# The output projection as a plain product over quarters of x1, with its sums on VectorE

## The chip, the core and the metric

The kernel runs on one core of one Trainium2 chip. The metric is the device time of one execution in microseconds (us). The engines are PE (TensorE matmuls; PEld is its weight loads), DVE (VectorE), ACT (ScalarE), POOL (GpSimd) and SP (SyncE, which here issues every DMA). Each engine takes its instructions in one fixed order, which a list scheduler made when the kernel was built.

## What is computed

One layer of a decoder trunk over 1024 tokens of width 1024, all float32. Three gated mixers give y; then come the output projection and a feed-forward part:

```python
y = gates[..., 0, :] * o_mla + gates[..., 1, :] * o_gla + gates[..., 2, :] * o_mem
x = x + y @ w_o                                          # the output projection
h2 = rms_norm(x, g_ffn)
return x + jnp.square(jax.nn.relu(h2 @ w_up)) @ w_down   # 1024 -> 4096 -> 1024
```

Every float32 product is made of three matmuls over rounded parts: an operand is split into `hi` (a cast by ACT, line 135) and `lo` (the difference, a subtraction by DVE, line 136), and the three are hi·hi, hi·lo and lo·hi.

## The kernel before

The change lies at the seam between the memory branch, whose last matmuls are the tiles `om` (line 131), the output projection (`phase_out`) and the first column groups of the up product (`phase_up`). Tokens lie on the partitions in tiles of 128, so x has 8 tiles; y lies transposed, as 8 tiles `Y` of 128 features by 1024 tokens. `x1` is x plus half of y @ w_o.

**Projection.** y @ w_o is a product of 2 x 2 blocks of 512 x 512, made as seven block products in Winograd's form instead of eight: step s is product `order[s]`, adds into a PSUM bank per token tile (`multiply`, line 1292: 4 tiles x 4 feature tiles x 3 matmuls = 48 matmuls), and after each step DVE adds half of the bank to a quarter of x1 (line 1296). The operands of most products are sums of blocks of y or w_o. They are formed by POOL (`tt`, lines 1237 to 1263), then split by ACT and DVE into slots. Four banks are used for four token tiles at a time, so a step can only begin in a fresh bank when that bank's sum has been taken over.

**Turning.** As quarters of x1 are complete, `scale` (lines 1304 to 1311) gets each token's factor by ACT and POOL and scales the tokens, `turn` (lines 1320 and 1333) turns them by PE and ACT, and `split` makes the operands of the up product: "11", "22", "21", "t1", "t2", "t3", "t4".

**Up product.** It runs by groups of 256 columns of w_up, again with seven products p1 to p7 per group (`up_group`, line 1460, 12 matmuls of 512 columns each). The first three groups are interleaved in `phase_up`, since their later operands are ready last. Weights of a group come by two DMAs into `fraw` (three buffers, line 1418); four sums of their blocks are formed (`up_weights`, lines 1430 to 1443), then split. In a group p6 leaves a sum in bank b2; DVE takes it over (`fu`, line 1496) before p7 may add more into the same bank; then DVE makes `fv` and `fc` (lines 1501 and 1503) before p3 may add into b3.

Of the kernel before, what the change touches and what calls it, by code (L numbers as in the profile page):

```python
# [7 lines left out]
F32 = mybir.dt.float32  # L8
# [11 lines left out]
P = 128  # L20
S = 1024
D = 1024
# [79 lines left out]
class _Kernel:  # L102
# [1101 lines left out]
    def phase_out(self):  # L1204
# [8 lines left out]
        Y, W, T = self.Y, {}, {}  # L1213
        places = {"12": ["wraw", "wraw", "whi", "wlo"], "21": ["whi"] * 4, "22": ["wlo"] * 4, "11": ["ftmp"] * 4}
        for n in ("12", "21", "22", "11"):
            for k in range(4):
                r = W[n, k] = self.t512(places[n][k])
                i, j = int(n[0]) - 1, int(n[1]) - 1
                nc.sync.dma_start(r, wv[4 * j + k][:, so[i]])
        order = (2, 5, 3, 1, 6, 7, 4)  # L1220
        goes = {1: (0, 0), 5: (1, 1), 6: (0, 1), 3: (0, 1), 7: (1, 1), 2: (0, 0), 4: (1, 0)}
        fresh = (2, 5, 1)
        A, C = {}, {}
        plan = {0: (False, False), 1: (True, True), 2: (True, False), 3: (False, True), 4: (True, True),
                5: (False, False), 6: (True, True)}
        tt = pool.tensor_tensor

        def conv_act(s, ks):
            i = order[s]
            if s not in A:  # L1230
                A[s] = self.slots(plan[s][0])
            h, l = A[s]
            for k in ks:
                y11, y12, y21, y22 = Y[k][:, so[0]], Y[k][:, so[1]], Y[4 + k][:, so[0]], Y[4 + k][:, so[1]]
                if i == 5:
                    src = self.t512("flo")
                    tt(src, y12, y11, op=ALU.subtract)
                elif i == 6:
                    tt(y12, y22, y12, op=ALU.subtract)
                    tt(y11, y12, y11, op=ALU.add)  # L1240
                    src = y11
                elif i == 4:
                    tt(y21, y21, y11, op=ALU.subtract)
                    src = y21
                else:
                    src = {3: y22, 2: y21, 1: y11, 7: y12}[i]
                self.split_sb(h[:, k, :], l[:, k, :], src)

        def conv_w(s, ks):
            i = order[s]  # L1250
            if s not in C:
                C[s] = self.slots(plan[s][1])
            h, l = C[s]
            for k in ks:
                if i == 5:
                    src = T["s", k] = self.t512("fhi")
                    tt(src, W["21", k], W["22", k], op=ALU.add)
                elif i == 3:
                    s2 = T["s", k]
                    tt(s2, s2, W["11", k], op=ALU.subtract)  # L1260
                    src = self.t512("flo")
                    tt(src, W["12", k], s2, op=ALU.subtract)
                    tt(W["21", k], W["11", k], W["21", k], op=ALU.subtract)
                else:
                    src = T["s", k] if i == 6 else W[{2: "12", 1: "11", 7: "21", 4: "22"}[i], k]
                self.split_sb(h[:, k, :], l[:, k, :], src)

        conv_act(0, range(4))
        conv_w(0, range(4))
        conv_act(1, range(4))  # L1270
        x1 = []
        for t2 in range(4):
            xt = self.hp.tile([P, 2, D], F32, name="x1", tag="H", bufs=8)
            for i in range(2):
                nc.sync.dma_start(xt[:, i, :], a["x"][0, (2 * t2 + i) * P:(2 * t2 + i + 1) * P, :])
                x1.append(xt[:, i, :])
# [4 lines left out]
        banks = {}  # L1281

        def multiply(s, p):
            i = order[s]
            if i in fresh:
                banks[p] = self.bank([P, 512], ("x1", "x2")[p // 2])
            ps = banks[p]
            (ah, al), (wh, wl) = A[s], C[s]
            tok = slice(P * p, P * p + P)
            for k in range(4):  # L1290
                for m, (l, r) in enumerate(((ah, wh), (ah, wl), (al, wh))):
                    pe.matmul(ps, l[:, k, tok], r[:, k, :], start=(i in fresh and k + m == 0), stop=(k == 3 and m == 2),  # L1292
                              skip_group_check=i not in fresh)
            oh, th = goes[i]
            acc = x1[4 * th + p][:, so[oh]]
            dve.scalar_tensor_tensor(acc, ps, 0.5, acc, op0=ALU.mult, op1=ALU.add)
# [42 lines left out]
        N = len(order)  # L1339
# [24 lines left out]
        at(5, 0, begin, ("11", True))  # L1364
        for k in range(4):
            at(5, k // 2, lambda k=k: split("11", k, raw[0, 0, k]))
            at(5, 2 + k // 2, second, k)
        at(6, 0, begin, ("t1", False), ("22", False), ("t3", False))
        at(6, 0, spill, range(4, 8))
        for k in range(4):  # L1370
            at(6, k // 2, lambda k=k: split("t1", k, raw[0, 0, k]))
            at(6, 2 + k // 2, third, k)
        for s in range(N):
            for p in range(4):
                multiply(s, p)
                if p < 2:
                    if s + 1 < N:
                        conv_w(s + 1, (2 * p, 2 * p + 1))
                elif s + 2 < N:
                    conv_act(s + 2, (2 * p - 4, 2 * p - 3))  # L1380
                for f in extra.get((s, p), []):
                    f()
        scale(1, 0, (0, 1))
        scale(1, 0, (2, 3))
        spill(range(4))
        begin(("t2", True), ("21", True), ("t4", False))
# [3 lines left out]
        def last():  # L1390
            for k in range(4):
                split("t2", k, raw[0, 0, k])
# [7 lines left out]
    def up_part(self, g, i, w):  # L1400
# [7 lines left out]
        if i == 5:  # L1408
            self.pool.tensor_tensor(r[0], r[0], r[1], op=ALU.add)
        w[i] = self.ff_split(r[0])  # L1410

    def up_weights(self, g, w=None):
# [10 lines left out]
        tt = self.pool.tensor_tensor  # L1423
# [107 lines left out]
    def phase_up(self, a_dram, close):  # L1531
# [9 lines left out]
        with tc.tile_pool(name="f_tmp", bufs=1, side="right") as tmp:  # L1541
# [16 lines left out]
            for i in (6, 7):  # L1558
                g0[i]()
            self.up_weights(1, w1)  # L1560
            for i in (4, 3):
                g0[i]()
            for i in (6, 7):
                g1[i]()
            self.up_weights(2, w2)
            for i in (4, 3):
                g1[i]()
            w = self.up_weights(3)
            for i in (6, 5, 7, 4, 3):
                g2[i]()  # L1570
            for g in range(3, NG):
# [253 lines left out]
```

## Time and profile before

| | |
|---|---|
| median of 3 runs | 1960.88 us (1959.6 to 1961.91) |
| the profiled execution | 1963.93 us, of which the span of its trace is 1962.1 us |
| mean granted TensorE clock of that execution | 0.988 of full speed |
| PE busy | 1894.0 us, 97% of the span |
| DVE, ACT, POOL busy | 1222.1, 901.6 and 563.1 us |
| DMA | 185.83 MB, 95 GB/s over the span |

All times of rows are counted from the start of the span. "Busy" of PE counts each matmul from its start to its modelled end, so that overlapping matmuls count once. Where an engine sat idle, the trace names what ended the idle time.

### The profile page before, as it was taken

Reading aid. Unit: us, or ns where it says so; the run is one execution under the profiler, and the core shown is the slowest. Engines: PE = TensorE matmul, PEld = TensorE weight load, DVE = VectorE, ACT = ScalarE, POOL = GpSimd, SP = SyncE. Lnnn points to the kernel's source line nnn. Section 1 sums busy time; section 2 is a strip of 40 time slices with the busy share of each in tenths; the row PEclk is TensorE's granted clock in tenths of the full one; section 3 lists DMA queues with packets and bytes.
Section 4 is the critical chain, followed back from the end, with each engine's and each line's share of the span. In section 5 each row is a group of like instructions: output and inputs, shape, how many; then the busy total and the mean of one; then the engine's idle time right before and its main releaser. Section 6 shows DMA issues by size and latency. Waiting matters only on the chain. (4 is left out here: it accounts for less than half of the span.)

```text
span 1962.1 us, 28464 instructions
## 1 busy us (share of the span) xinstructions
PE 1894.0 (97%) x10330; PEld 1627.2 (83%) x10330; DVE 1222.1 (62%) x2125; ACT 901.6 (46%) x2125; POOL 563.1 (29%) x644
## 2 busy tenths in 40 slices
PE   7999999999999999999999998898999999999999
PEld 6889989899879798888988987576888887888887
DVE  7666464655656636364455446876756567698796
ACT  5465465554653323233244434375444546544432
POOL 2321313112124323232310125723322224244150
PEclk9999999999999999999999999899999999999999
DMA  4021110211111411112123114034545457745543
GB/s 144 25 65 49 30 52 28 62 47 48 38 55 34 139 44 43 43 44 73 31 62 113 43 36 150 17 118 124 182 135 161 141 166 247 241 131 187 182 137 118
DMA packets 141852, 185.83 MB, mean 95 GB/s; under 512 B 11352, under 2 KB 91744, under 8 KB 141712
## 3 DMA queue, kind: packets, MB, share of 16 engines
q1 hardware_dynamic: 141712, 184.02, 29.7%
q8 instruction: 81, 1.33, 0.3%
q14 instruction: 59, 0.48, 0.1%
HBM read 137.84 MB, written 46.14 MB: 94 GB/s over the span
## 5 line engine op out<-in xcount | busy, mean ns | idle before, releaser
L208 PE MATMUL mm<-H,whi 128*128 128x512 f32 x1280 | 411.2, 400 | 2.2 <-DVE g_rg L767 2.2
L208 PEld LDWEIGHTS mm<-H,whi 128*128 128x128 f32 x1280 | 232.5, 190 | 42.4 <-DVE g_rg L767 2.6
L208 PE MATMUL mm<-H,wlo 128*128 128x512 f32 x640 | 253.3, 396 | 0.0
L136 DVE TENSOR_TENSOR wlo<-wraw,whi 128x768 fp32r<-128x768 f32 (+3 forms) x134 | 113.4, 850 | 119.9 <-ACT whi L135 116.8
L208 PEld LDWEIGHTS mm<-H,wlo 128*128 128x128 f32 x640 | 121.1, 189 | 24.8
L135 ACT CAST whi<-wraw 128x768 fp32r<-128x768 f32 (+3 forms) x134 | 95.9, 721 | 94.0 <-PE mm L208 42.2
L131 PE MATMUL s<-whi,H 128*128 128x384 f32 x512 | 139.1, 346 | 0.0
L1679 PE MATMUL x<-h,h 128*128 128x512 f32 x528 | 121.8, 390 | 0.0
L1679 PEld LDWEIGHTS x<-h,h 128*128 128x128 f32 x528 | 99.1, 188 | 21.0
L221 PE MATMUL mm<-whi,H 128*128 128x256 f32 x512 | 95.7, 285 | 0.0
L131 PEld LDWEIGHTS s<-whi,H 128*128 128x128 f32 x512 | 93.4, 188 | 1.0 <-ACT whi L135 0.2
L1460 PE MATMUL b<-H,whi 128*128 128x512 f32 x272 | 86.9, 401 | 5.6 <-DVE fc L1503 4.3
L131 PE MATMUL s<-wlo,H 128*128 128x384 f32 x256 | 87.6, 342 | 0.2 <-DVE wlo L136 0.2
L221 PEld LDWEIGHTS mm<-whi,H 128*128 128x128 f32 x512 | 80.8, 192 | 0.3
L1460 PE MATMUL b<-h,whi 128*128 128x512 f32 x248 | 78.4, 396 | 1.1 <-ACT whi L135 1.1
L1460 PE MATMUL b<-H,fhi 128*128 128x512 f32 x240 | 74.5, 391 | 2.5 <-DVE fc L1503 2.5
L823 ACT ACTIVATE g_dd<-g_dd 128x1024 f32<-128x1024 f32 x28 | 29.6, 1058 | 100.1 <-POOL g_dd L822 100.1
L1687 DVE TENSOR_TENSOR acc<-x,acc 128x512 f32<-128x512 f32 x80 | 54.2, 683 | 32.6 <-PE x L1679 32.4
L221 PE MATMUL mm<-wlo,H 128*128 128x256 f32 x256 | 72.4, 283 | 0.0
L586 DVE TENSOR_REDUCE sst<-s 128x1 f32<-128x384 f32 (+4 forms) x96 | 52.8, 554 | 31.3 <-PE s L584 18.0
L1679 PE MATMUL x<-H,h 128*128 128x512 f32 x288 | 68.2, 395 | 0.0
L1679 PE MATMUL x<-h,H 128*128 128x512 f32 x288 | 68.1, 395 | 0.0
(455 smaller groups left out, 5064.4 us busy)
## 6 DMA issues: line engine op xcount, KB each, us to landing
wraw<-w_in SPq DMA_DIRECT2D x58, 384.0 KB, 3.4
a<-fc SPq DMA_DIRECT2D x80, 256.0 KB, 2.8
fraw<-w_up SPq DMA_DIRECT2D x32, 512.0 KB, 4.4
whi<-a SPq DMA_DIRECT2D x56, 256.0 KB, 4.0
wlo<-a SPq DMA_DIRECT2D x56, 256.0 KB, 3.8
x<-x SPq DMA_DIRECT2D x24, 512.0 KB, 5.8
dw<-x SPq DMA_DIRECT2D x32, 256.0 KB, 3.4
a<-wraw SPq DMA_DIRECT2D x30, 256.0 KB, 2.1
```

The lines of the kernel that those rows point to most:

```text
L131: self.pe.matmul(out, l, r, start=(i == 0), stop=(i == last))
L135: self.act.copy(hi, src)
L136: self.dve.tensor_tensor(lo, src, hi.bitcast(F32), op=ALU.subtract)
L208: self.pe.matmul(ps, l[:, c], r[:, tok], start=(k + i == 0), stop=(k == KT - 1 and i == 2))
L221: self.pe.matmul(ps[:, i, :], l[:, tok], r, start=(k + j == 0), stop=(k == KT - 1 and j == 2))
L586: self.dve.tensor_reduce(st[:, b:b + 1], sp[b][:, 0:n], axis=X, op=ALU.max, negate=True)
L823: act.activation(dd, dd, AF.Exp, scale=0.0625)
L1460: pe.matmul(ps[name], l[:, k, :], r[:, k, :], start=(not more and k + m == 0), stop=(k == 3 and m == 2), skip_group_check=more)
L1679: pe.matmul(ps, l[:, k, tok], r[:, k, :], start=(i in (1, 5, 2) and k + m == 0), stop=(k == 3 and m == 2), skip_group_check=i not in (1, 5 ...
L1687: dve.tensor_tensor(out, ps, out, op=ALU.add)
```

## The change

The projection becomes a plain product: eight steps instead of seven, each one half of the sum for a quarter of x1 (512 output columns by 512 tokens). Two steps follow each other in the same four banks, and DVE adds the banks to x1 only after the second. The operands are blocks of y and of w_o as they are; POOL forms no sums for them any more. The x1 tiles lie in the buffers of `Y`, the y operands keep the eight `H` slots. The scaling and turning of a quarter moves with its step. The sums for the up product's weights (in `up_part`, and in `up_weights` for the first three groups) and the one in `third` go from POOL to DVE. In `phase_up` the call that makes the next group's weights stands behind the products p6, p7, p4, p3 of the group before, where it stood between p7 and p4, so it has a lower priority than their evictions.

```diff
+        def weights(n):
+            i, j = int(n[0]) - 1, int(n[1]) - 1
+            r = [self.t512({"11": "wraw", "12": "fhi", "22": "ftmp", "21": "flo"}[n]) for _ in range(4)]
             for k in range(4):
...
+                nc.sync.dma_start(r[k], wv[4 * j + k][:, so[i]])
+            if n == "11":
+                W[n] = [[x[:, 0, :] for x in self.ff_split(x.unsqueeze(1))] for x in r]
+                return
+            hi, lo = self.slots(True)
...
+        def tokens(kh, th):
+            hi, lo = Y[kh, th] = self.slots(False)
+            for k in range(4):
+                self.split_sb(hi[:, k, :], lo[:, k, :], self.Y[4 * kh + k][:, so[th]])
...
+        weights("11")
+        tokens(0, 0)
+        tokens(0, 1)
...
+        load_x1(range(4))
+        tokens(1, 0)
+        weights("12")
+        tokens(1, 1)
+        load_x1(range(4, 8))
+        weights("22")
+        weights("21")
...
+        steps = [(oh, th, kh) for oh, th, khs in ((0, 0, (0, 1)), (0, 1, (0, 1)), (1, 1, (1, 0)), (1, 0, (0, 1))) for kh in khs]
 
         def multiply(s, p):
-            i = order[s]
-            if i in fresh:
+            oh, th, kh = steps[s]
+            first = s % 2 == 0
+            if first:
                 banks[p] = self.bank([P, 512], ("x1", "x2")[p // 2])
...
+            if not first:
+                acc = x1[4 * th + p][:, so[oh]]
+                dve.scalar_tensor_tensor(acc, ps, 0.5, acc, op0=ALU.mult, op1=ALU.add)
...
-        for s, (oh, th) in ((4, (0, 0)), (5, (0, 1)), (6, (1, 1))):
+        for s, (oh, th) in ((2, (0, 0)), (4, (0, 1)), (6, (1, 1))):
...
-            tt(r12, r22, r12, op=ALU.subtract)
-            split("t3", k, r12)
+            dve.tensor_tensor(r12, r22, r12, op=ALU.subtract)
...
-            self.pool.tensor_tensor(r[0], r[0], r[1], op=ALU.add)
+            self.dve.tensor_tensor(r[0], r[0], r[1], op=ALU.add)
...
-        tt = self.pool.tensor_tensor
+        tt = (self.dve if had else self.pool).tensor_tensor
...
-            for i in (6, 7):
+            for i in (6, 7, 4, 3):
                 g0[i]()
             self.up_weights(1, w1)
-            for i in (4, 3):
-                g0[i]()
-            for i in (6, 7):
+            for i in (6, 7, 4, 3):
                 g1[i]()
             self.up_weights(2, w2)
-            for i in (4, 3):
-                g1[i]()
-            w = self.up_weights(3)
             for i in (6, 5, 7, 4, 3):
                 g2[i]()
+            w = self.up_weights(3)
```

The scheduler decides where this puts the instructions. On POOL, behind the last additions of the memory branch (`Y<-Y,m_y`), these rows stood before:

```order
L1237 TENSOR_TENSOR flo<-Y 128x512 [waits Pool_49] x2
L1138 TENSOR_TENSOR Y<-Y,m_y 128x512 [waits DVE_49]
L1237 TENSOR_TENSOR flo<-Y 128x512 [waits Pool_49]
L1257 TENSOR_TENSOR fhi<-whi,wlo 128x512 [waits DMAHW5_49,DMAHW4_49]
...
L1263 TENSOR_TENSOR whi<-ftmp,whi 128x512 [waits DMAHW1_49,Pool_49]
...
L1260 TENSOR_TENSOR fhi<-fhi,ftmp 128x512 [waits DVE_49]
L1239 TENSOR_TENSOR Y<-Y 128x512
L1262 TENSOR_TENSOR flo<-wraw,fhi 128x512 [waits DMAHW0_49,Pool_49]
```

Now the additions are followed by the small operations of `scale` alone:

```order
L1138 TENSOR_TENSOR Y<-Y,m_y 128x512 [waits DVE_49] x14
L1279 TENSOR_TENSOR f_q<-f_q,xms 128x2 [waits PE_49,Activation_49]
L1280 TENSOR_SCALAR f_q<-f_q 128x2 [waits Pool_49]
L1281 TENSOR_TENSOR f_sc<-f_q,mhalf 128x2 [waits Pool_49]
```

The 32 block sums of the projection are gone from POOL, and the last addition of the memory branch has no sum ahead of it. On SP, whose queue issues the loads, the second quarter of w_o (`fhi`, for the second step) now stands behind loads of x and of w_up:

```order
L1376 DMA wraw<-w_up 128x4x128 [waits DMAHW3_49,DVE_49]
L1242 DMA Y<-x 128x1024 [waits DVE_49,Pool_49]
L1242 DMA Y<-x 128x1024 [waits DVE_49] x2
L1376 DMA wraw<-w_up 128x4x128 [waits DMAHW4_49,DVE_49,Activation_49]
L1219 DMA fhi<-w_o 128x512 [waits DMAHW5_49,PE_49]
```

Before, the last quarter to be loaded (`ftmp`) stood behind loads of x alone:

```order
L1275 DMA x_12877<-x 128x1024 [waits DMAHW7_49]
L1275 DMA x_12880<-x 128x1024 [waits DMAHW0_49]
L1219 DMA ftmp<-w_o 128x512 [waits DVE_49,DMAHW1_49,PE_49,Activation_49]
L1219 DMA ftmp<-w_o 128x512 [waits DMAHW2_49]
```

So the load of `fhi` can't be issued until a buffer of `wraw` is free. On DVE, where group 0's p6 is taken over (`fu<-fs,b`), the order before was this; the four rows ahead of it split group 0's weights, and the sums are POOL's:

```order
L136 TENSOR_TENSOR flo<-ftmp,fhi 128x512
L136 TENSOR_TENSOR wlo<-ftmp,whi 128x512
L136 TENSOR_TENSOR flo<-fraw,fhi 128x512
L136 TENSOR_TENSOR wlo<-ftmp,whi 128x512
L1496 TENSOR_TENSOR fu<-fs,b_13872 128x512
```

Now, from the first of group 1's sums on (lines 1399, 1401, 1408 and 1412 are the four sums of a group):

```order
L1399 TENSOR_TENSOR ftmp<-fraw 128x512
L1401 TENSOR_TENSOR ftmp<-ftmp,fraw 128x512
L1408 TENSOR_TENSOR ftmp<-fraw 128x512
L1412 TENSOR_TENSOR ftmp<-fraw,ftmp 128x512
L136 TENSOR_TENSOR flo<-ftmp,fhi 128x512
L136 TENSOR_TENSOR wlo<-ftmp,whi 128x512
L136 TENSOR_TENSOR flo<-fraw,fhi 128x512
L136 TENSOR_TENSOR wlo<-ftmp,whi 128x512
L1399 TENSOR_TENSOR ftmp<-fraw 128x512
L1465 TENSOR_TENSOR fu<-fs,b_13818 128x512
L1401 TENSOR_TENSOR ftmp<-ftmp,fraw 128x512
```

Ahead of group 0's `fu` there stand now, besides group 0's own sums and splits, those of group 1 and the first sum of group 2, which waits for group 2's load.

## Rows read from the trace of the kernel before

**Rows 1.** The page: span, and PE's busy time, share and instructions.

```profile
span 1962.1 us, 28464 instructions
PE 1894.0 (97%) x10330; PEld 1627.2 (83%) x10330; DVE 1222.1 (62%) x2125; ACT 901.6 (46%) x2125; POOL 563.1 (29%) x644
```

**Rows 2.** Three stretches: projection, first three groups, later groups; columns named in row one.

```profile
core 0: us, PE busy (x) PEld busy (x) DVE busy (x) ACT busy (x) POOL busy (x), PEclk, DMA share, GB/s
1204.33:1317.55 113.22, 97.40 (x399) 74.40 (x398) 87.16 (x103) 54.09 (x106) 65.77 (x52) 0.91 0.28 98
1317.55:1395.09 77.54, 66.68 (x271) 51.60 (x270) 55.62 (x73) 43.46 (x76) 32.54 (x23) 0.93 0.44 139
1395.09:1560.00 164.91, 164.91 (x718) 134.48 (x717) 102.83 (x138) 80.20 (x135) 49.68 (x35) 1.00 0.48 152
```

**Rows 3.** PE's waits, 1204 to 1317.5: us in total, times, longest.

```profile
PE x L1292 <- DVE h L136: 4.7, 2, 4.4
PE x L1292 <- DVE x L1296: 3.8, 2, 2.7
PE x L1292 <- ACT H L135: 3.2, 2, 2.3
PE trs L1320 <- ACT ftmp L1311: 2.1, 2, 1.8
PE om L131 <- ACT m_ph L1124: 0.6, 1, 0.6
```

**Rows 4.** PE's instructions in order of time: start, us, line, tiles, count, idle before.

```profile
1226.10 13.25 PE L1292 MATMUL x<-h,h 128*128 128x512 f32 x44 [0.28 <-DVE h L136]
...
1304.04 1.04 PE L1320 MATMUL trs<-ident,ftmp 128*128 128x128 f32 x8
1304.83 8.47 PE L1292 MATMUL x<-h,h 128*128 128x512 f32 x36
...
1363.65 0.70 PE L1460 MATMUL b<-H,whi 128*128 128x512 f32 x2 [3.86 <-DVE fc L1503]
...
1368.07 0.63 PE L1460 MATMUL b<-h,fhi 128*128 128x512 f32 x2
```

**Rows 5.** DVE in order of time: a split beside POOL's sums, and with POOL idle.

```profile
1216.51 6.17 DVE L136 TENSOR_TENSOR h<-flo,h 128x512 fp32r<-128x512 f32 x4 [4.36 <-ACT h L135]
...
1268.07 2.48 DVE L136 TENSOR_TENSOR h<-fhi,h 128x512 fp32r<-128x512 f32 x4
```

**Rows 6.** POOL in order of time: the last two additions to Y.

```profile
1209.54 1.29 POOL L1138 TENSOR_TENSOR Y<-Y,m_y 128x512 f32<-128x512 f32 x1 [2.55 <-DVE m_y L1136]
...
1214.54 1.29 POOL L1138 TENSOR_TENSOR Y<-Y,m_y 128x512 f32<-128x512 f32 x1
```

**Rows 7.** DVE in order of time: the last m_y of the memory branch.

```profile
1210.87 0.69 DVE L1136 SCALAR_TENSOR_TENSOR m_y<-m_gate,om 128x512 f32<-128x512 f32 x1 [1.41 <-POOL Y L1138]
```

**Rows 8.** SP's issues in order of time: w_o, then fraw.

```profile
1209.98 1.94 SPq L1219 DMA_DIRECT2D ftmp<-w_o  x4
...
1340.04 1.05 SPq L1418 DMA_DIRECT2D fraw<-w_up  x2
```

**Rows 9.** DMA issues, 1170 to 1235: line, count, KB each, median us to landing.

```profile
ftmp<-w_o SPq DMA_DIRECT2D x4, 256.0 KB, 4.0
```

**Rows 10.** The loads of fraw, 1336 to 1400.

```profile
DMA to landing us min/median/max: 3.7/4.4/7.7
```

**Rows 11.** POOL in order of time: the first sum of group 0's weights.

```profile
1346.98 1.29 POOL L1430 TENSOR_TENSOR ftmp<-fraw 128x512 f32<-128x512 f32 x1 [23.77 <-DMA fraw<-w_up]
```

**Rows 12.** DVE, then ACT: the last read of Y's buffers; copies out of banks.

```profile
1337.41 0.68 DVE L1396 TENSOR_TENSOR flo<-flo,Y 128x512 f32<-128x512 f32 x1
...
1328.26 1.84 ACT L1333 ACTIVATE Y<-trs,vec 128x512 f32<-128x512 f32 x3 [1.42 <-PE trs L1320]
```

**Rows 13.** PE's waits, 1317.5 to 1395.1.

```profile
PE b L1460 <- DVE fc L1503: 4.3, 2, 3.9
PE trs L1320 <- ACT ftmp L1311: 2.8, 1, 2.8
```

More of the change, by code (lines that the diff above doesn't have):

```diff
@@ L1212, in phase_out @@
         so = [slice(0, 512), slice(512, 1024)]
[L1213 to L1215 removed]
+        T, Y, W = {}, {}, {}
+        def weights(n):
+            i, j = int(n[0]) - 1, int(n[1]) - 1
+            r = [self.t512({"11": "wraw", "12": "fhi", "22": "ftmp", "21": "flo"}[n]) for _ in range(4)]
             for k in range(4):
[L1217 to L1219 removed]
@@ L1220, in phase_out @@
[L1220 to L1228, printed above, removed]
-            i = order[s]
[L1230 to L1276, printed above, removed]
+                nc.sync.dma_start(r[k], wv[4 * j + k][:, so[i]])
+            if n == "11":
+                W[n] = [[x[:, 0, :] for x in self.ff_split(x.unsqueeze(1))] for x in r]
+                return
@@ new lines, in weights @@
+            hi, lo = self.slots(True)
+            W[n] = [(hi[:, k, :], lo[:, k, :]) for k in range(4)]
+            for k in range(4):
+                self.split_sb(*W[n][k], r[k])
+        def tokens(kh, th):
+            hi, lo = Y[kh, th] = self.slots(False)
+            for k in range(4):
+                self.split_sb(hi[:, k, :], lo[:, k, :], self.Y[4 * kh + k][:, so[th]])
+        self.fams = ["w"]
+        weights("11")
+        tokens(0, 0)
+        tokens(0, 1)
+        x1 = [None] * NT
@@ L1277, in phase_out, with load_x1 @@
+        def load_x1(ts):
+            for t in ts:
+                x1[t] = self.new_Y(F32)
+                nc.sync.dma_start(x1[t], a["x"][0, t * P:(t + 1) * P, :])
+        load_x1(range(4))
[5 more added lines that the diff above has]
+        weights("21")
         sm = self.small
@@ L1281, in phase_out @@
         banks = {}
+        steps = [(oh, th, kh) for oh, th, khs in ((0, 0, (0, 1)), (0, 1, (0, 1)), (1, 1, (1, 0)), (1, 0, (0, 1))) for kh in khs]
         def multiply(s, p):
-            i = order[s]
-            if i in fresh:
+            oh, th, kh = steps[s]
+            first = s % 2 == 0
+            if first:
                 banks[p] = self.bank([P, 512], ("x1", "x2")[p // 2])
             ps = banks[p]
-            (ah, al), (wh, wl) = A[s], C[s]
+            ah, al = Y[kh, th]
             tok = slice(P * p, P * p + P)
-            for k in range(4):
+            for k, (wh, wl) in enumerate(W[f"{oh + 1}{kh + 1}"]):
                 for m, (l, r) in enumerate(((ah, wh), (ah, wl), (al, wh))):
[L1292 to L1296, printed above, removed]
+                    pe.matmul(ps, l[:, k, tok], r, start=(first and k + m == 0), stop=(not first and k == 3 and m == 2))
+            if not first:
+                acc = x1[4 * th + p][:, so[oh]]
+                dve.scalar_tensor_tensor(acc, ps, 0.5, acc, op0=ALU.mult, op1=ALU.add)
         def scale(oh, th, js):
@@ L1337, in spill @@
                 nc.sync.dma_start(self.x_dram[t], x1[t])
-        N = len(order)
+        N = len(steps)
         extra = {}
@@ L1363, in begin @@
                 B[n] = self.slots(own)
-        at(5, 0, begin, ("11", True))
-        for k in range(4):
[L1366 to L1369, printed above, removed]
+        at(4, 0, begin, ("11", True))
+        at(5, 1, begin, ("t1", False))
+        at(6, 0, spill, range(4, 8))
+        at(6, 0, begin, ("22", False))
+        at(7, 0, begin, ("t3", False), ("t2", True))
+        for k in range(4):
+            at(4, 2 + k // 2, lambda k=k: split("11", k, raw[0, 0, k]))
+            at(5, k // 2, second, k)
+            at(5, 2 + k // 2, lambda k=k: split("t1", k, raw[0, 0, k]))
+            at(6, 2 + k // 2, third, k)
+            at(7, k // 2, lambda k=k: split("t3", k, raw[0, 1, k]))
+            at(7, 2 + k // 2, lambda k=k: split("t2", k, raw[0, 0, k]))
         for k in range(4):
-            at(6, k // 2, lambda k=k: split("t1", k, raw[0, 0, k]))
-            at(6, 2 + k // 2, third, k)
+            at(7, k, scale, 1, 0, (k,))
         for s in range(N):
@@ L1390, in last @@
         def last():
-            for k in range(4):
-                split("t2", k, raw[0, 0, k])
             for k in range(4):
```

9 lines of the change are left out of this document (1 added, 8 removed).

## The prediction, made before the changed kernel was run

> **What bounds the kernel now.** I read the page first: PE is busy for 1894.0 of 1962.1 us [rows 1], so what counts is where PE idles or runs slowly. The view by stretches finds it at the seam that the change touches. In the later groups of the up product 718 matmuls take 164.91 us at full granted clock [rows 2]: 0.2297 us each, the price of one 512-column matmul when nothing waits. A batch of 8 turns takes 0.79 us, from 1304.04 to the next matmul at 1304.83 [rows 4]: 0.099 us each. At these prices the two stretches ahead of it are worth:
>
> - Stretch A, the projection from 1204.33 to 1317.55: 336 projection matmuls, 12 of the memory branch, 48 turns: 348 x 0.2297 + 48 x 0.099 = 84.7 us. It takes 113.2, so 28.5 are lost.
> - Stretch B, the first three groups to 1395.09: 252 matmuls and 16 turns: 59.5 us. It takes 77.5, so 18.0 are lost.
>
> PE's waits name the causes in A: splits by DVE and casts by ACT of operands that POOL sums late, evictions (line 1296) queued behind slow splits, scaled tokens that come late [rows 3]. The four largest rows sum to 13.8 us. Most of the rest is slow matmuls: the granted clock averages 0.91 in A [rows 2], and right after a wait 44 matmuls take 13.25 us where the price is 10.1, so 3 us more [rows 4]. In B the largest waits are 4.3 and 2.8 us [rows 13], at a mean granted clock of 0.93.
>
> PE has no such idle time in the stretch behind B, so I take a microsecond won or lost up to there for one at the end.
>
> **The change, part by part.**
>
> *The eighth step.* 48 more matmuls: 48 x 0.2297 = +11.0 us on PE. Nothing hides it.
>
> *The 32 sums of POOL that go.* Off PE, so no gain of their own; but they are what A's operands wait for. A second effect: a split by DVE took 6.17/4 = 1.54 us beside them and 2.48/4 = 0.62 with POOL idle [rows 5]. I take 0.62 for every DVE operation on 512 columns and 0.52 to 0.61 for one of ACT (three copies in 1.84 us [rows 12]). The Trainium skill ("SBUF — State Buffer", section Who interferes with whom) says that a DVE instruction with two SBUF inputs and a GpSimd instruction that reads SBUF exclude each other for a whole instruction. The trace agrees in direction; by full exclusion a split would cost its own 0.62 plus a POOL addition of 1.29 [rows 6], 1.9 us, more than the 1.54 seen, and the sum below would not change.
>
> *Are the new operands in time?* Step 0 needs y blocks finished long before and w_o's first quarter, like the first step before. It keeps the 0.6 us wait of `om` [rows 3] and ends at 1204.3 + 0.6 + 60 x 0.2297 = 1218.7. Step 1 needs the second quarter of w_o, whose load stands behind a wait for a `wraw` buffer. The last w_o load before went out at 1209.98 [rows 8], when the memory branch's storage came free; I take the same time, since the buffer is free after the last early splits, about 1209. With 4.0 us to landing [rows 9] and four issues in 1.94 us, it is there from 1214 to 1216. ACT reaches these casts after the last y block: the last m_y ended at 1211.6 [rows 7]; the addition, 1.29 us, was done only at 1215.8, since POOL had sums ahead of it [rows 6]; now it ends at 1212.9, its cast at 1213.6. So four casts and splits make step 1's operands by 1214.9 to 1217.3, ahead of 1218.7. If they came late, the price is that of the present wait, 4.4 [rows 3] and 3 for slow matmuls after it [rows 4]: 7.4. I take 0.
>
> *Evictions and turns in A.* Half as many bank evictions (16 for 28), each 0.7 us behind splits of 0.62. A fresh bank of a step pair is needed 11 us after its predecessor's first token tile was finished. Each quarter's last eviction has 36 matmuls, 8.3 us, ahead of the turn that needs it; eviction, two ACT operations and POOL's three small ones take about 5. So A becomes 84.7 + 11.0 + 0.6 = 96.3 us: **16.9 us less**, and up to 7.4 worse.
>
> *B: the seam to the groups.* Call the end of the last projection step T. PE then has 12 matmuls, 16 turns, and 84 matmuls whose operands come before: 96 x 0.2297 + 1.6 = 23.7 us; then p6 of group 0 (12) and 7 of p4, 4.4 us: PE reaches p7 at T + 28.1. p7 adds into p6's bank, so it must wait for `fu`. That is DVE's row behind group 1's four sums and splits and group 2's first sum. Its time:
>
> - `fraw` lies in Y's storage, so its first load waits for the last read of the turned tiles. From T: the last eviction (0.8), scaling (0.7), then the turn behind the 12 matmuls: first bank ready at T + 3.3, first copy at T + 4.0. From there DVE has 4 subtractions and 7 of 8 splits to the last one that reads such a tile, 11 x 0.62: T + 10.9. Before, that read ended at 1338.09 [rows 12], 20.5 us behind the end of A.
> - The two loads of group 0: issued by T + 11.5. Before, the issue was at 1340.04 or soon after [rows 8] and POOL's wait ended at 1346.98 [rows 11], 6.5 us with three loads in flight. So T + 18.0.
> - Group 0's first three sums, 2.05, free the first buffer; group 1's second load takes 4.4, the median [rows 10]; three sums, 2.1, free the third buffer; group 2's load 4.4; its first sum and `fu` 1.4: 14.4.
>
> So `fu` ends at T + 32.4: PE waits **4.3 us** where it waited 3.9 + 1.3 for evictions and 2.8 for turns. After a wait of 3.86 us twelve matmuls took 4.42 us, 1363.65 to 1368.07 [rows 4], 1.7 more than their price; I add that, and 1.0 for small waits. B becomes 59.5 + 4.3 + 1.7 + 1.0 = 66.5: **11.0 us less**. At the shortest landing, 3.7 [rows 10], three landings shrink by 4.2 and the wait is about 0; at the longest, 7.7, they grow by 7.8 and it is 12. With 3 for slow matmuls B lies between 59.5 and 74.7.
>
> *The sums moved to DVE.* 12 for the groups, 4 in `third`, 2 in `up_part`: 18 x 0.62 = 11 us more on DVE, which was busy for 87 us of A and 56 of B [rows 2], much of the first beside POOL's sums. They hide under PE except where counted above; that they don't is a rival.
>
> **The sum.** 16.9 + 11.0 = 27.9 us off. The profiled execution took 1963.93, 1.83 more than its span and 3.05 more than the median; the difference holds for either, so the forecast for the median is 1960.9 - 27.9 = **1933**. With A at 96.3 to 103.7 and B at 59.5 to 74.7, the gain is 35 to 12.4: 1926 to 1948.5.
>
> **The rivals.**
>
> 1. *No wait at p7.* The loads land sooner than I took, or `fraw` need not wait so long, so DVE is never late. For it: a landing of 3.7 is in the rows. Against it: three in a row would have to be short. B is 59.5 to 61.5: 1926 to 1928.
> 2. *A stays ragged.* Late w_o or casts blocked by a slot make a second stall at step 1 or a turn: 7.4 us each, one or two of them: 1940 to 1948. For it: SP's queue has w_up's load, which waits, ahead of w_o's; against it the 1.4 to 3.8 us of slack above.
> 3. *DVE becomes the bound.* If DVE had no room, the 18 sums would delay PE by their whole time, 11 us: 1944. For it: DVE's order is fixed and dense in B. Against it: with POOL's sums gone each split in A is 0.9 us shorter, and DVE had 22 us free in B [rows 2]. The Trainium skill ("Perfetto Trace Analysis", section Optimizing Scalar/DVE Operations) would take work off a saturated VectorE, even onto GpSimd, the reverse of this edit; the trace shows no saturated VectorE here.
> 4. *Slower: DVE holds the groups up.* If the sums of each next group's weights stood in front of the evictions in all three groups and each load took about 7 us, p7 would wait some 10 us per group and the matmuls behind it 3 more: 39 us in B, against 34.9 that A and B together can give: 1965. It decides from landings of 7 us on in every group. Against it: only group 0's `fu` has the blocked row ahead of it in DVE's order, and the median landing is 4.4.
> 5. *It changes nothing.* The 11.0 us of extra matmuls would have to meet unchanged waits in one stretch and a gain of 11 in the other: 1957 to 1965.
>
> **Chances.** The forecast, 1928 to 1940, 0.60; rival 1, 0.14; rival 2, 0.13; rival 3, 0.04; between 1948 and 1957, 0.02; rival 5, 0.03; rival 4, 0.04. The range 1926 to 1944 leaves out about 0.17: half of rival 2, what lies above it, and a little below. A difference under 0.2%, 3.9 us, can't be told from none in this kernel. Faster: 0.60 + 0.14 + 0.13 + 0.04 + 0.02 = 0.93; same 0.03; slower 0.04.
>
> **What would show it.** After: 97 us or so from PE's first projection matmul to the first of group 0, with a granted clock near 1.00 and no wait for DVE or ACT over 1 us; DVE's splits at 0.62 there; POOL idle but for the factors. In B one wait of PE for `fu` (line 1465) of 2 to 7 us, ended by a DVE row behind a sum that waited for `fraw`, and slow matmuls behind it. I am wrong if A shows a wait at step 1, if p7 doesn't wait, or if the clock in A stays near 0.9 without waits.

## Result: 1961.0 to 1934.3 us, and the profile after

The kernel before took 1961.01 us (median of four runs, 1959.6 to 1961.91), the changed one 1934.31 us (four runs, 1932.61 to 1935.1): ratio 0.9863, 95% interval 0.9846 to 0.988, so 26.7 us less. The forecast was 1933, range 1926 to 1944. The profiled execution took 1935.1 us with a span of 1933.2, 28.9 less than the span in [rows 1].

The page's span and the rows of PE and POOL:

```profile
span 1933.2 us, 28442 instructions
PE 1890.7 (98%) x10378; PEld 1630.5 (84%) x10378; DVE 1180.2 (61%) x2107; ACT 890.0 (46%) x2101; POOL 486.9 (25%) x594
```

The same two stretches as in [rows 2], with the same columns: A from PE's first matmul of the projection to the first of group 0, B from there to the first of group 3:

```profile
1203.66:1302.33 98.67, 97.51 (x448) 79.37 (x447) 49.35 (x77) 45.06 (x85) 10.73 (x16) 1.00 0.32 111
1302.33:1364.61 62.28, 60.52 (x269) 48.76 (x268) 46.13 (x71) 35.78 (x62) 11.16 (x8) 1.00 0.55 176
```

A went from 113.22 to 98.67 us (14.6 less, with 48 matmuls more), B from 77.54 to 62.28 (15.3 less). The granted clock is 1.00 in both, where it was 0.91 and 0.93. PE starts on the projection 0.67 us earlier, and behind B 1.6 us are given back: 14.55 + 15.26 + 0.67 - 1.58 = 28.9.

PE's waits in A, the whole list (the kernel before has seven kinds, five of them in [rows 3]):

```profile
PE om L131 <- ACT m_ph L1124: 1.2, 1, 1.2
```

ACT, then DVE, in order of time: w_o's second quarter cast and split for step 1 (the casts but for the first, then all four splits). Then SP's issues of that quarter and of the first `fraw` loads:

```profile
1216.48 1.82 ACT L135 CAST h<-fhi 128x512 fp32r<-128x512 f32 x3 [1.52 <-DMA fhi<-w_o]
```

```profile
1215.08 0.68 DVE L136 TENSOR_TENSOR h<-fhi,h 128x512 fp32r<-128x512 f32 x1
1217.13 1.90 DVE L136 TENSOR_TENSOR h<-fhi,h 128x512 fp32r<-128x512 f32 x3 [1.37 <-ACT h L135]
```

```profile
1210.02 1.75 SPq L1219 DMA_DIRECT2D fhi<-w_o  x4
...
1313.21 10.47 SPq L1387 DMA_DIRECT2D fraw<-w_up  x5
```

PE in order of time: step 1 and the matmul after it, then the last of p4's seven, p7's first and the matmul after p7:

```profile
1218.94 11.36 PE L1267 MATMUL x<-h,H 128*128 128x512 f32 x48
1230.14 0.39 PE L1267 MATMUL x<-whi,H 128*128 128x512 f32 x1
...
1330.81 0.39 PE L1429 MATMUL b<-H,fhi 128*128 128x512 f32 x1
1332.96 0.70 PE L1429 MATMUL b<-H,whi 128*128 128x512 f32 x2 [1.76 <-ACT fhi L135]
...
1335.80 0.39 PE L1429 MATMUL b<-H,fhi 128*128 128x512 f32 x1
```

DVE in B: the first sums of groups 0, 1 and 2 (line 1399), and `fu` (line 1465) behind the third:

```profile
1318.81 0.69 DVE L1399 TENSOR_TENSOR ftmp<-fraw 128x512 f32<-128x512 f32 x1 [3.02 <-DMA fraw<-w_up]
...
1324.89 0.69 DVE L1399 TENSOR_TENSOR ftmp<-fraw 128x512 f32<-128x512 f32 x1 [1.04 <-DMA fraw<-w_up]
...
1331.52 0.69 DVE L1399 TENSOR_TENSOR ftmp<-fraw 128x512 f32<-128x512 f32 x1 [1.58 <-issue]
1332.13 0.68 DVE L1465 TENSOR_TENSOR fu<-fs,b 128x512 f32<-128x512 f32 x1
```

`fu` ends at 1332.81 and p7 starts at 1332.96, 2.15 us behind the matmul before it, which costs 0.23: a wait of 1.9 us at the place foretold. The view names ACT's cast into `fhi` as the releaser; that cast and `fu` end within 0.15 us of each other, so the row can't decide (e5 and e11 do). For the wait ahead of group 2's first sum the view names no releaser (`issue`); that group's load was issued at 1326.94, 4.6 us before the sum began, and the loads of `fraw` around it took 3.8 to 5.8 us to land.

The 1.6 us given back lie at the end of the up product. There PE waits about 2.5 us in both kernels ahead of the last group's last product; its twelve matmuls took, before and then after, as stretches (the granted clock is the third number from the right):

```profile
1646.40:1649.26 2.86, 2.86 (x12) 2.36 (x13) 1.15 (x2) 2.42 (x4) 0.00 (x0) 1.00 0.75 274
```

```profile
1615.92:1620.36 4.44, 4.44 (x12) 3.50 (x13) 1.15 (x2) 2.41 (x4) 0.00 (x0) 0.62 0.62 207
```

### The profile page after: what moved, and what is told of

The parts are those of the page before. It is cut to its first block, busy times and chain, and to the rows that moved or that the text cites. A ratio compares the mean times of both kernels' runs of the same rounds, so it can differ in the third digit from the quotient of the medians.

```text
span 1933.2 us, 28442 instructions
## 1 busy us (share of the span) xinstructions
PE 1890.7 (98%) x10378; PEld 1630.5 (84%) x10378; DVE 1180.2 (61%) x2107; ACT 890.0 (46%) x2101; POOL 486.9 (25%) x594
## 4 chain that ended last, share of the span: by engine, by line
PE 81%; DVE 3%; ACT 1%; DMA 1%; POOL 1%; issue 1%; SPq 0%; DVEq 0%; ACTq 0%; POOLq 0%
PE mm L208 20%; PE x L1644 16%; PE b L1429 14%; PE s L131 5%; PE x L1267 5%; PE mm L221 5%; PE s L581 3%; PE pv L131 2%; PE gram L857 2%; PE km L131 1%; PE tr L615 1%; PE qm L131 1%; PE go L131 1%; PE om L131 1%; DMA fraw<-w_up 1%
## 5 line engine op out<-in xcount | busy, mean ns | idle before, releaser
L135 ACT CAST whi<-wraw 128x768 fp32r<-128x768 f32 (+3 forms) x138 | 98.6, 719 | 90.9 <-PE mm L208 42.7
L1267 PE MATMUL x<-h,H 128*128 128x512 f32 x288 | 68.6, 397 | 0.0
```

The lines of the kernel that those rows point to most:

```text
L135: self.act.copy(hi, src)
L1267: pe.matmul(ps, l[:, k, tok], r, start=(first and k + m == 0), stop=(not first and k == 3 and m == 2))
```

## The experiments

The theory: A's loss hung on POOL's sums (operands late, splits slowed beside POOL, clock lost behind the waits), and without them one wait at p7 stays, for `fu`. The rivals: DVE is the bound; the groups' own edits, not the projection, shortened B; POOL's work beside DVE's, and not its lateness, made A ragged (contention). Times are medians; ratios are to the kernel before on the same chip, with the 95% interval. A and B are as above.

**The four parts apart.** e1 puts the moved sums back on POOL, e2 restores the order of the groups, e3 keeps the new projection alone, e4 the groups' edits alone:

```diff
 # e1: changed kernel, and POOL in three places
-            self.dve.tensor_tensor(r[0], r[0], r[1], op=ALU.add)
+            self.pool.tensor_tensor(r[0], r[0], r[1], op=ALU.add)
-        tt = (self.dve if had else self.pool).tensor_tensor
+        tt = self.pool.tensor_tensor
-            dve.tensor_tensor(r12, r22, r12, op=ALU.subtract)
+            pool.tensor_tensor(r12, r22, r12, op=ALU.subtract)
 # e2: changed kernel, and phase_up as before
 # e3: changed kernel, and up_part, up_weights, phase_up as before
 # e4: kernel before, and up_part, up_weights, phase_up as changed
```

> The changed kernel with its moved sums put back on POOL: the 12 of the first three groups, the 2 of group 0's and 1's part 5, and 4 of the third operand. Theory (the sums' engine matters only through the time at which fu is done, and that hangs on the landings): POOL's sums take about 1.29 us where DVE's take 0.62, three of them stand between two landings of fraw, so fu comes some 2 to 4 us later than T + 30.5 and PE waits 3 to 6 us at p7 instead of 1.8; stretch A stays at 98 to 100 us; 1935 to 1940 us. Rival (DVE is the bound, and the 18 sums delay PE by their own 11 us): with the sums off DVE the kernel gets faster, 1923 to 1930. Second rival (the sums on DVE are what brought B its gain): B goes back to some 77 us, 1949.

> The changed kernel with the program order of the first three groups as before the change: the weights of group 1 between p7 and p4 of group 0, those of group 2 between p7 and p4 of group 1, those of group 3 ahead of group 2's steps. Theory (the rank of evictions against the next group's weights moves nothing that PE waits for, since DVE's rows up to fu stand in the same order): within 3 us of the changed kernel, 1932 to 1937. Rival (the rank is what shortened B): B loses most of its 15 us, 1943 to 1950.

> The new projection alone (third's four sums on DVE with it), with the weights' sums on POOL and the order of the groups as before the change. Theory (A's gain belongs to the projection, and most of B's too, since the seam's turns, splits and evictions are done earlier and the clock does not fall): A 98 to 100 us, B 64 to 68 us, 1935 to 1941. Rival (B's 15 us come from the edits in the groups): A 98 to 100, B 75 to 78, 1947 to 1951.

> The old projection with the edits of the groups alone: weights' sums on DVE, evictions ranked ahead. Theory (as before: B's gain is the seam's): A stays at 113 us, B at 73 to 79 us, 1957 to 1963. Rival (B's 15 us come from the edits in the groups): B about 62 us, 1944 to 1948.

| kernel | us | ratio | A | B |
|---|---|---|---|---|
| before (profile) | 1961.0 | | 113.2 | 77.5 |
| changed (profile) | 1934.3 | 0.9863 (0.9846 to 0.988) | 98.7 | 62.3 |
| e1 | 1939.7 | 0.9894 (0.9879 to 0.9909) | 98.6 | 68.6 |
| e2 | 1936.9 | 0.9878 (0.9863 to 0.9893) | 98.7 | 65.2 |
| e3 | 1940.6 | 0.99 (0.9886 to 0.9914) | 98.6 | 68.7 |
| e4 | 1951.4 | 0.9963 (0.9948 to 0.9977) | 109.5 | 69.2 |

The projection alone is worth 1.00%, the groups' edits alone 0.37%, and both 1.37%: they add up. In e3, A is whole and B is 8.8 us shorter than before (expected 64 to 68); in e4, B is 8.3 us shorter, which I had put down to the seam, and A 3.7, which I had not expected. So neither theory nor rival for B was right alone: about half of B's gain is the projection's and half the groups'. PE's waits in B sum to 10.9 us in the kernel before and to 5.4 in e3, so waits are 5.5 of the projection's 8.8 us. e1 is not faster, which rival 3 needs: its fastest run, 1937.2 us, is longer than the slowest of the changed kernel. So DVE is not the bound; and e1 equals e3 within the noise, so what the groups' edits are shown to bring is the sums' engine. Why POOL costs there: DVE in e1, ahead of `fu`, and PE at p7:

```profile
1329.31 1.10 DVE L136 TENSOR_TENSOR flo<-ftmp,fhi 128x512 fp32r<-128x512 f32 x1 [3.85 <-ACT fhi L135]
1330.55 1.53 DVE L136 TENSOR_TENSOR wlo<-ftmp,whi 128x512 fp32r<-128x512 f32 x1
...
1333.21 0.67 DVE L1465 TENSOR_TENSOR fu<-fs,b 128x512 f32<-128x512 f32 x1
```

```profile
1333.94 1.22 PE L1429 MATMUL b<-H,whi 128*128 128x512 f32 x2 [4.55 <-DVE fu L1465]
1334.95 0.63 PE L1429 MATMUL b<-H,wlo 128*128 128x512 f32 x1
```

Group 1's splits wait for sums that POOL makes late, `fu` stands behind them, PE waits 4.55 us, and its matmuls run slowly behind the wait: p7's twelve take 5.14 us, 1333.94 to 1339.08, at a granted clock of 0.52. That is 4.6 - 1.8 of wait and 5.1 - 2.8 of pace: 5.1 of the 6.3 us by which B is longer.

e2's interval and that of the changed kernel overlap; no effect of the rank on the time is shown. DVE's rows up to `fu` stand in the same order. Of the 2.9 us that its B is longer, 0.8 are a wait for group 2's `fu` and 1.6 are slow matmuls behind p7's wait of 1.92 us, which took 4.42 us for 2.84:

```profile
1335.09 1.07 PE L1429 MATMUL b<-H,whi 128*128 128x512 f32 x2 [1.92 <-ACT fhi L135]
1335.96 0.63 PE L1429 MATMUL b<-H,wlo 128*128 128x512 f32 x1
```

**e10: where e4's 3.7 us in A come from.** Only `up_part`'s two sums move to DVE in the kernel before:

```diff
-            self.pool.tensor_tensor(r[0], r[0], r[1], op=ALU.add)
+            self.dve.tensor_tensor(r[0], r[0], r[1], op=ALU.add)
```

> The kernel before with one edit alone: the two sums of up_part (part 5 of groups 0 and 1) on DVE and not on POOL. Theory (in the run of the groups' edits alone A was 109.5 and not 113.2 us, because these two sums stand ahead of a scaling's factors in POOL's order and wait for loads of w_up): A 109 to 110 us, the wait of 1.84 us ahead of the turns at 1298 gone, B 76 to 78; 3 to 4.5 us less than the kernel before, ratio 0.9977 to 0.9985. Rival (A was shortened by the other edits, or by chance): A 112 to 114, ratio 0.999 to 1.001.

Ratio 0.999 (0.9981 to 0.9998), 1957.9 us; A 110.6, B 75.8. The mechanism is the one expected, but the effect is smaller: the ratio is outside the expected 0.9977 to 0.9985 and touches the rival's range, A is just above its 109 to 110 and B just below its 76 to 78. POOL in the kernel before, with one of `up_part`'s two sums (line 1409) between two steps of a scaling's factors:

```profile
1293.86 0.53 POOL L1305 TENSOR_TENSOR f_q<-f_q,xms 128x2 f32<-128x2 f32 x1 [6.15 <-ACT f_junk L1304]
1294.67 1.28 POOL L1409 TENSOR_TENSOR wraw<-wraw 128x512 f32<-128x512 f32 x1 [0.28 <-DMA wraw<-w_up]
1296.04 0.55 POOL L1306 TENSOR_SCALAR f_q<-f_q 128x2 f32<-128x2 f32 x1
```

In e10 and e4 the turns that waited 2.1 us for the scaled tokens in [rows 3] wait for nothing. The twelve matmuls behind those turns took 4.42 us in the kernel before, at a granted clock of 0.61, and 2.86 in e4: 2.1 + 1.6 is all of e4's 3.7. e10 lost 1.45 of that again in another place: behind an eviction's wait of 2.72 us, which the kernel before has too, twelve matmuls took 4.33 us at 0.63, and 2.88 at 1.00 in the kernel before.

**e7: the kernel before without its projection's sums.**

```diff
                 if i == 5:
-                    src = self.t512("flo")
-                    tt(src, y12, y11, op=ALU.subtract)
+                    src = y12
 ...
                 if i == 5:
-                    src = T["s", k] = self.t512("fhi")
-                    tt(src, W["21", k], W["22", k], op=ALU.add)
+                    src = T["s", k] = W["22", k]
 # and so for the other sums of conv_act and conv_w
```

> The kernel before with its projection's 32 sums on POOL left out: each step splits one of the tiles that its sum would have read, so the seven products are of the wrong operands; loads, splits, matmuls, evictions and turns stay in number. Theory (A's loss comes from operands that POOL sums late and from splits slowed beside POOL, and the clock falls because of these waits): A falls from 113 to 87 to 92 us, splits take 0.62 us, the granted clock in A is 0.97 or more; 1936 to 1943 us. Rival (A's loss belongs to the seven-product plan itself: its 28 evictions and 28 banks, whatever the sums do): A stays at 104 us or more, 1952 us or more.

1935.0 us, ratio 0.9875 (0.9862 to 0.9889). Its two stretches:

```profile
1202.86:1290.91 88.05, 85.87 (x399) 70.25 (x397) 64.97 (x102) 53.15 (x106) 15.77 (x20) 1.00 0.35 126
1290.91:1365.87 74.96, 65.52 (x271) 50.66 (x270) 55.59 (x74) 43.47 (x76) 32.03 (x22) 0.95 0.45 144
```

A falls by 25.2 us with all 336 matmuls, 28 evictions and 48 turns in place, and the clock stands at 1.00: the sums made A ragged, not the seven-product plan. Against A of the changed kernel, 98.67, the eighth step costs 10.6.

**e8 and e8b: lateness or contention?** Both add POOL work that nobody reads to the changed kernel's projection. In e8 it depends on nothing, in e8b on the evictions:

```diff
 # e8, behind each token tile's matmuls
+                for _ in range(4):
+                    pool.tensor_tensor(z, z, z, op=ALU.add)
 # e8b instead, behind each eviction into acc
+                for i in range(4):
+                    pool.tensor_tensor(z, z, acc[:, P * i:P * i + P], op=ALU.add)
```

> The changed kernel with 128 additions of 128 columns on POOL in the projection (4 behind each token tile's matmuls, on a tile that nothing else reads). It tells lateness from contention: POOL is as busy as before but nobody waits for its results. Theory (a DVE split beside POOL's additions takes longer, up to 1.5 us, but DVE has the room while operands are not late): splits' mean rises to 0.8 to 1.3 us, A stays below 101 us, time within 3 us of the changed kernel. Rival (the contention is what made A ragged): A 104 us or more, 1939 us or more.

> The changed kernel with 64 additions of 128 columns on POOL in the projection, four behind each eviction, each reading what the eviction wrote, so that they come spread over steps 1, 3, 5 and 7 and none piles up ahead of the factors of the scaling; nothing reads their result. At 0.45 us each they keep POOL busy for 29 us of the projection, where the changed kernel has it busy for 11 and the kernel before for 66. Theory (contention with POOL lengthens DVE's instructions, but PE does not wait while no operand hangs on POOL): A 98 to 101 us, DVE's splits and evictions longer by up to 0.3 us in the mean, time within 3 us of the changed kernel. Rival (contention alone makes A ragged): A 104 us or more, 1939 us or more.

e8 took 1965.7 us, 1.0032 (1.002 to 1.0044), with A at 130.5. By its numbers the rival had won, but the rows name another cause. PE's longest wait, then POOL:

```profile
PE trs L1296 <- ACT ftmp L1287: 28.2, 2, 17.4
```

```profile
1215.48 37.71 POOL L1357 TENSOR_TENSOR f_z<-f_z 128x128 f32<-128x128 f32 x70
1253.15 0.19 POOL L1281 TENSOR_TENSOR f_q<-f_q,xms 128x2 f32<-128x2 f32 x1
```

Seventy of the additions were ordered in a row, and the first scaling's factors, 0.19 us of work, stood behind them: lateness again, by a queue. Apart from the waits of those turns PE waited for no split and no eviction, with POOL busy for 67.7 us of A. e8b spreads the additions: 1935.9 us, 0.9877 (0.9859 to 0.9895), A 99.2 with POOL busy for 40 us of it (from an execution of 1940.96 us, one of two of the five that took 1941; its B, 65.0, has a wait of 2.9 us at p7). The splits of w_o's last quarter take 0.88 us in the mean, against 0.68 in the changed kernel, and PE waits 0.3 us for the turns. So 0.5 us of A for 30 us of POOL work beside it: contention of this size alone doesn't make A ragged.

But the sums of the kernel before were of 512 columns and slowed a split to 1.54 us [rows 5], and there the slowing itself set waits. PE, ACT and DVE in the kernel before:

```profile
1224.40 1.41 PE L1292 MATMUL x<-h,h 128*128 128x512 f32 x3 [4.42 <-DVE h L136]
```

```profile
1218.82 0.62 ACT L135 CAST h<-fhi 128x512 fp32r<-128x512 f32 x1 [0.77 <-POOL fhi L1257]
```

```profile
1222.60 3.44 DVE L136 TENSOR_TENSOR h<-fhi,h 128x512 fp32r<-128x512 f32 x2
```

The split that ended A's longest wait had its sum and its cast by 1219.44, but began at 1222.60, because four slow splits ahead of it kept DVE busy from 1216.51 on. At their price with POOL idle these would have taken 3.7 us less (6.17 - 2.48), so most of that wait is the price of contention and not of a late sum: an estimate, which no run tried. The eviction behind the wait of 2.7 us also stood behind four such splits, 6.27 us from 1257.07. The waits for ACT's casts into `H`, 3.2 us, are for late sums. e7 takes both causes away at once, so how its 25.2 us divide between lateness and contention stays open.

**e5 and e11: p7's wait.** e5 puts group 2's sums on POOL; e11 leaves them on DVE, but writes the first of them where group 0's `u1` lies, which is free only behind `fv`:

```diff
 # e5
-        tt = (self.dve if had else self.pool).tensor_tensor
+        tt = (self.dve if had and g < 2 else self.pool).tensor_tensor
 # e11
-        s1 = new()
+        if g == 2:
+            s1 = self.tmp.tile([P, 512], F32, name="fs", tag="fs", bufs=2).rearrange("p (k n) -> p k n", k=4)
+        else:
+            s1 = new()
```

> The changed kernel with the four sums of group 2's weights alone on POOL; in DVE's order fu then stands ahead of everything that waits for group 2's loads. Theory (p7 of group 0 waits for fu, and fu stands behind group 2's first sum, which waits for a landing): PE's gap of 2.15 us ahead of p7 is gone or below 0.5, B is about 60.3 us instead of 62.3, and the time is some 2 us below the changed kernel's: 0.983 to 0.986 of the kernel before. Rival (p7 waits for ACT's cast into fhi, which the view of waits names as the releaser): the gap stays at 1.8 us or so and the time is the changed kernel's.

> The changed kernel with the first sum of group 2's weights written into a buffer that group 0's u1 holds until fv is done, so that DVE's order is fu, fv, the first row of part 4, and only then group 2's sums; these stay on DVE. Theory (p7 waits for fu behind that sum): PE's gap ahead of p7 is below 0.5 us, no other wait over 1 us comes in the groups, since group 2's weights are wanted some 15 us later; B 59.8 to 60.8 us, 0.984 to 0.986 of the kernel before. Rival (the delay only moves: group 2's splits or casts are late for group 1's or 2's products): a wait of 2 us or more further on and B 62 us or more.

In both, p7's wait is gone (no wait in e5, 0.25 us in e11) with nothing changed about the cast that the view had named: p7 waited for `fu`. But neither gains: e5 1938.5 us, 0.9889 (0.9876 to 0.9903), B 66.9; e11 1934.6 us, 0.9867 (0.9851 to 0.9883), B 64.8. The wait moved on. DVE, then PE, in e11:

```profile
1347.96 1.09 DVE L136 TENSOR_TENSOR wlo<-ftmp,whi 128x512 fp32r<-128x512 f32 x1 [2.22 <-ACT whi L135]
1348.98 0.68 DVE L1475 TENSOR_TENSOR fc<-fv,b 128x512 f32<-128x512 f32 x1
```

```profile
1349.71 0.74 PE L1432 MATMUL b<-H,whi 128*128 128x512 f32 x2 [2.39 <-DVE fc L1475]
```

A split of group 2's weights now stands ahead of group 1's `fc` and waits for ACT; in e5 it is `fv` and `fc` of group 0 behind splits that wait for POOL, and PE waits 3.3 us. As long as DVE makes the next weights and the evictions in one order, the delay goes to the next eviction.

**e9 and e12: where operands lie.** In A, step 1's 48 matmuls took 11.20 us, 0.2333 each, where the price from [rows 2] is 0.2297. The y operands lie in the pool `H`, three quarters of w_o in the pool `h2` (`h` in the rows). e9 lays both operands of six steps in one pool, e12 those of four, together with e11's edit (the pools of the turned operands that follow change with them):

```diff
 # e9 (e12: "12", "11", "10" in h2)
+        own = {n: self.slots(n in ("21", "01", "00")) for n in ("01", "00", "21", "12", "11", "10", "22")}
-            hi, lo = self.slots(True)
+            hi, lo = own[n]
-            hi, lo = Y[kh, th] = self.slots(False)
+            hi, lo = Y[kh, th] = own[f"{kh}{th}"]
```

> The changed kernel with the projection's operands laid so that in six of the eight steps both operands lie in the same pool (two token quarters and w_o's quarter 21 in h2, the others in H), where they all lay in different ones. In the trace of the changed kernel a matmul whose operands lie in different ones of these pools takes 0.234 us (48 in 11.2), and the steps of the kernel before with both in one pool take 0.228. Theory (the pace goes with where the two operands lie): 288 matmuls at 0.228 instead of 0.234, A shorter by 1.5 to 2.0 us, 96.6 to 97.2 us; time down by as much. Rival (the pace goes with something else, the kind of step or the engines beside it): A 98.3 us or more.

> The same, and the projection's operands laid so that four of the eight steps have both operands in one pool (w_o's quarter 12 and the token quarters of the second half of y in h2, the rest in H), without the late start in h2 that cost e9 its 3.7 us. Theory (pace by place, 0.228 against 0.234 us a matmul): 192 matmuls save 1.2 to 1.5 us, A 97.2 to 97.6 us, no wait at step 1; with B as in the run above 0.983 to 0.985 of the kernel before, some 3 us below the changed kernel. Rival (h2 comes free too late for step 1): a wait at step 1 of 2 us or more and A 100 us or more.

PE in order of time, 84 matmuls and the turn after them, in e9 and then in e8, where the operands lie as in the changed kernel:

```profile
1253.35 19.34 PE L1268 MATMUL x<-H 128*128 128x512 f32 x84
1272.53 1.03 PE L1295 MATMUL trs<-ident,ftmp 128*128 128x128 f32 x8
```

```profile
1274.75 19.85 PE L1269 MATMUL x<-h,H 128*128 128x512 f32 x84
1294.44 1.04 PE L1296 MATMUL trs<-ident,ftmp 128*128 128x128 f32 x8
```

19.18 against 19.69 us: 0.2283 and 0.2344 each. The pace goes with the place. Which mix is slow shows in B of the changed kernel, where the other operand lies in a third pool (`whi`, `wlo`), each row being two of three matmuls:

```profile
1309.28 0.63 PE L1429 MATMUL b<-h,whi 128*128 128x512 f32 x2
...
1309.98 0.63 PE L1429 MATMUL b<-h,whi 128*128 128x512 f32 x2
...
1313.46 0.61 PE L1429 MATMUL b<-H,whi 128*128 128x512 f32 x2
...
1314.14 0.61 PE L1429 MATMUL b<-H,whi 128*128 128x512 f32 x2
```

Three matmuls of `h2` with `whi` or `wlo` take 0.70 us, three of `H` with them 0.68. So two pools are not slow by that alone: slow are the mixes of `h2` with another pool.

e9 as a whole is slower than the changed kernel, 1938.1 us, 0.9895 (0.9882 to 0.9909): ACT casts step 0's tokens into h2 late, and PE waits 3.7 us for them, with slow matmuls behind it; A, counted from the same place, is 103.8 us. e12 has no such wait:

```profile
1204.08:1300.50 96.42, 96.42 (x448) 79.21 (x445) 49.27 (x79) 46.46 (x89) 9.26 (x16) 1.00 0.32 113
1300.50:1363.67 63.17, 60.58 (x270) 48.76 (x269) 46.08 (x71) 34.91 (x62) 13.35 (x8) 1.00 0.54 174
```

A is 2.25 us shorter than the changed kernel's: 192 x 0.0061 = 1.2 by the pace, and the 1.2 us wait of `om` is gone, which was not foreseen. B is 0.9 longer, with e11's wait for `fc`, 2.5 us. 1933.0 us, 0.9858 (0.9842 to 0.9874): the best of the ratios, but its interval overlaps nearly all of the changed kernel's, so no better version is shown.

## Why the prediction was right, point by point

The forecast was 27.9 us less; it was 26.7 by the medians and 28.8 between the profiled executions. In these, two terms were mis-sized in opposite directions, A's gain by -2.3 us and B's by +4.3, and 1.6 were given back behind B. That the sum came so close is in part luck.

- *The eighth step*, +11.0: step 1, one of the new kind, takes 11.2. By e7 against the changed kernel, 10.6. Right.
- *The 32 sums of POOL that go*: right, and shown by e7, for lateness and slowed splits together. The splits' 0.62 us is right too (in A they follow one another at 0.61).
- *Are the new operands in time?* Issue foretold at 1209.98, made at 1210.02. But three of the four casts had to wait until 1216.48 for their tiles, foretold for 1214 to 1216, and the last split ended at 1219.03, not by 1217.3: by the prediction's own measure the slack was gone, since step 1 began at 1218.94. There was no wait, so the value taken, 0, held, with the help of room that it had not counted: a token tile goes through the four feature tiles in turn, three matmuls each, so the fourth is wanted 9 x 0.233 = 2.1 us into the step (an estimate). In e8 the same splits ended 1.1 us into the step, and PE didn't wait either.
- *Evictions and turns in A*: no wait, as foretold; A 98.67 for 96.3, so its gain 14.6 and not 16.9. The term mis-sized is the price of a matmul: 288 of the projection's now have one operand in `H` and one in `h2`, and at 0.2344 for 0.2297 they cost 1.4 us more. The stretch up to step 1 took 15.3 us where its 60 matmuls and the wait of `om` were put at 14.4: `om` waited 1.2 for 0.6, and 0.3 went around that wait.
- *B: the seam to the groups*: the place, the row and the chain were right, and the sizes too long, most of all the first loads (5.6 us from issue to the first sum for 6.5). `fraw` was issued at T + 10.9 (T + 11.5 foretold), the first sum ran at T + 16.5 (18.0), `fu` ended at T + 30.5 (32.4), PE was at p7 at T + 28.7 (28.1). So PE waited 1.9 us, not 4.3, which is less than the 2 to 7 us named as the sign. And the clock held: p7's twelve matmuls took 2.84 us where I added 1.7 to their price of 2.76. That was luck, since in e2 they took 4.42 behind nearly the same wait. B is 62.3 for 66.5: its gain 15.3 and not 11.0.
- *The sums moved to DVE*: that they hide is right (rival 3 falls by e1), but I treated them as harmless only. By e1 they are worth 6.3 us of B, since DVE's chain to `fu` is shorter than POOL's would be. The forecast of B had it right without saying so, since its chain was worked out with DVE's sums.
- *No such idle time in the stretch behind B*: not quite. Both kernels have one wait of 2.5 us there, and the clock behind it gave back 1.6 us.

Rival 2 would have needed a late operand in A; e8 shows such a case, by a queue, at 32 us. Rival 4 needed long landings in all groups; e5 and e11 show its mechanism, a weight's row ahead of an eviction, at 2 to 3 us of wait. The Trainium skill ("SBUF — State Buffer", section Who interferes with whom) would have a VectorE instruction with two SBUF inputs and a GpSimd one that reads SBUF shut each other out; e1's split of 1.53 us beside POOL's sums, against 0.68, agrees in direction.

Open: how A's loss divides between late sums and slowed splits; what the 3.3 us of e3's gain in B that are not waits consist of; and whether the rank of the evictions brings anything.

## What to carry to other kernels

Weigh saved matmuls against what the sums that save them cost, in operands that come late and in other engines' work that they slow: here seven products with sums took 113 us, without the sums 88, and eight plain ones 99. On an engine that works in order, look for the smallest piece of work that somebody waits for, and at what stands ahead of it: one sum of 1.28 us ahead of a factor, or one ahead of an eviction, set PE's waits. Taking such a wait away moves it to the next eviction unless the order behind it has room too.

## What the runs showed of the hardware that was not expected

- The clock behind a wait of PE can't be told from the wait's length here. Behind the same wait of 2.72 us, for the same eviction, the granted clock was 1.00 in the kernel before and 0.63 in e10. It was full after waits of 1.76 (p7, changed kernel) and 2.54 us (end of the up product, before), and 0.61 to 0.63 after 1.92 (p7, e2), 2.39 (e11) and 2.53 us (end of the up product, changed kernel). After 3.29 us in e5 it was 0.50, the lower of TensorE's two levels (1.2 GHz); after 4.55 in e1, 0.52. Twelve matmuls behind these waits took 2.8 to 2.9 us at full clock and 4.3 to 5.3 us otherwise.
- A 512-column matmul takes 0.2283 us with both operands in `H` and 0.2344 with one in `H` and one in `h2`, with no wait in either (84 matmuls each, e9 and e8). In B of the changed kernel it is 0.233 with `h2` and a third pool, and 0.227 with `H` and that pool. The cause within the chip was not tried.
- POOL and DVE slow each other when both work on 512 columns: in the kernel before, four of POOL's sums took 6.76 us from 1217.04, beside DVE's splits, 1.7 each, and two that ran while DVE was idle (1212.05 to 1214.58) took 1.28 and 1.29; the splits took 1.54 for 0.62 [rows 5].
- PE reached the projection between 1202.45 and 1206.35 us in executions (e5, e8b) whose edits lie behind that point in the program. Differences of 2 us between the spans of two single executions say nothing; stretches counted from the same instruction do.
